# Down product of a gated MLP: seven operand slots, chunks of 3 to 4 pairs, another product order, three homes for h

## The chip, the cores and the metric

The kernel runs on one core of a Trainium2 chip. The metric is the device time of one execution in microseconds (us). Times of the whole program are medians of three runs; everything that is said about single instructions comes from one profiled execution.

Engine names are those of the profile: PE is TensorE (matrix products), DVE is VectorE, ACT is ScalarE, POOL is GpSimd, SP is SyncE, which here only issues DMA transfers. Each engine works through its own instruction list in order. A DMA transfer is issued by one of SP, ACT and POOL and then runs on the core's 16 DMA engines. In the profile, transfers issued by SP are on the queue "hardware_dynamic", those issued by POOL on "software_dynamic".

## What is computed

One decoder layer for 512 prompt positions and 64 sampled positions (576 columns in all). The change concerns the last part only, the gated MLP:

```
def conv_ffn(hn, prev_g, w_gate, w_up, conv_w, conv_b, w_down):
    g = hn @ w_gate                      # 2048 -> 5504
    u = hn @ w_up                        # 2048 -> 5504
    gp = concatenate([prev_g, g], axis=1)
    gc = conv_b + sum(conv_w[j] * gp[:, j:j + T] for j in range(3))
    return (silu(gc) * u) @ w_down       # 5504 -> 2048
...
y = h + conv_ffn(rms_norm(h, g_ffn), ...)
```

All tensors are float32. `h` is the residual stream after attention; it is added to the result.

## The kernel before

**Products in two parts.** A float32 operand is split into a high and a low float32r part (weights `wu`, `wl`; activations `xh`, `xl` or `hi`, `lo`). `multiply` forms wu·xh + wu·xl (lines L1638, L1639), then wl·xh (L1641), so three matmuls of 128x128 by 128x288 per block of 128 rows.

**Seven products for eight.** Gate, up and down use Strassen's scheme in Winograd's form on 2x2 blocks: seven products, numbered 1 to 7, in place of eight. Each needs a combination of the four weight blocks `a11, a21, a22, a12` and one of the activation blocks. `Weights.operand(i)` makes the weight combination: for product 5 the sum `s = a21 + a22` (L1918), then in place `a21 = a11 - a21` (L1919) and `a11 = s - a11` (L1920); for product 6 `s = a12 - a11` (L1924). Then ACT copies the result to `wu` (`upper`, L1626) and DVE subtracts for `wl` (`lower`, L1631). There are four buffers each of `wu` and `wl`, used in turn, so a combination can be made at most four products ahead. `ahead()` makes the next one in the list `todo`, once per product.

**Weight loads.** The four raw blocks of an item go through a ring of five buffers `wrs`, loaded by SP (L1621). `behind` says after which operand the next item's blocks are asked for: after product 1 `a11`, after 6 `a21`, after 7 `a22`, after 4 `a12`. A load into a ring buffer has to wait for the last reader of what was in it.

**Stages.** Gate/up: 43 items, one for each 128 columns of the 5504, each seven products (five for eight of them, whose other two were made earlier). After every second item, `pair` forms the seven activation combinations of the down product for that pair, splits each into a buffer `pp` (two buffers; ACT copy L196, DVE subtraction L199) and stores it to DRAM, `opd[i-1, pair]`, 288 KB, by a DMA issued on POOL (L1785). There are 21 pairs; the last item is odd and has no partner (`oddx`).

Down: the 21 pairs are cut into six chunks `CTS = (4, 4, 4, 3, 3, 3)`, numbered q = 0 to 5. For each chunk, four groups g of 256 output rows (128 from each of two subgroups s, in both row halves), so 24 items. Each item does the seven products for s = 0 and 1: a half product is 12 matmuls for four pairs and 9 for three. An activation operand `ops[q, i]` is loaded from `opd` (`fetch`, L1985, on POOL) into one slot, 1152 KB for four pairs or 864 KB for three, and used by all four groups; in group 3 each slot is free after its product, and the next operand in the list `coming` is loaded into it. The slots are the ten buffers of the gate/up activations that the last gate item frees first (`release(*xops[i])` for products 1, 5, 6, 3, 7).

After each half product, DVE adds the accumulator in PSUM to the rows of `ht` (L2111), which holds h and ends as the output. The PSUM banks are `a` for products 1, 6, 7 and 4 (`pgemm`), `b` for 5 and 3, `c` for 2 (`pone`).

**The hand-over.** Two ring and sum buffers, `room` and `sums`, lie in `x12`, and the scratch of the convolution in `x21`; both are freed together when gate/up ends. `ht` (36 KB in each partition) takes their place, so the last gate item and the first down item have special rules in `behind`, `ahead` stops at the end of the gate list, and a new sum buffer and a fifth ring buffer (`wr4`) are made. `ht` is loaded by eight DMAs on SP (L2060).

The order of instructions on each engine is set by a scheduler that simulates the program; the code gives data, buffers and the order of calls, and the scheduler may run a later instruction earlier.

Of the kernel before, what the change touches and what calls it, by code (L numbers as in the profile page):

```python
# [17 lines left out]
P = 128  # L18
# [29 lines left out]
CQA, CKA, CVA, CFA, CQB, CKB, CVB, CQI, CKI, CWI = (  # L48
    0, 1024, 2048, 3072, 3080, 4104, 4360, 4616, 5640, 5704)
NLATE = 5  # L50
CTS = (4, 4, 4, 3, 3, 3)
PRE = tuple(range(0, 24, 3))


# [1 line left out]
def tile_hymba_step(  # L56
# [1505 lines left out]
    wq_ctx, wq = opened("wq")  # L1562
    fn_ctx, fn = opened("fn")
    wb_ctx, wb = opened("wb")
    ha_ctx, hap = opened("ha", RIGHT)
    hb_ctx, hbp = opened("hb", RIGHT)


    x12, x21 = [hap.tile([P, 8, HALF], F32, name=n) for n in ("x12", "x21")]
    x11, x22 = [hbp.tile([P, 8, HALF], F32, name=n) for n in ("x11", "x22")]  # L1570
    xblk = ((x11, x12), (x21, x22))

# [207 lines left out]
    def pair(n, x, y):  # L1780

        def out(i, t):
            s = prp.tile([P, 2, HALF], F32R, name="pp", bufs=2)
            split(s[:, 0, :], s[:, 1, :], t)
            G.dma_start(opd[i - 1, n], f(s))  # L1785

        b11, b12, b21, b22 = x[:, HV[0]], x[:, HV[1]], y[:, HV[0]], y[:, HV[1]]
        ta, tb = [prp.tile([P, HALF], F32, name=n) for n in ("ta", "tb")]
        V.tensor_sub(ta, b22, b12)
        V.tensor_sub(tb, b12, b11)  # L1790
        out(1, b11)
# [100 lines left out]

    xops = {1: (hi11, lo11), 5: (hi1, lo1), 6: (hi2, lo2), 3: (hi22, lo22), 7: (hi3, lo3), 2: (hi21, lo21), 4: (hi4, lo4)}
    ORDER = (1, 5, 6, 3, 7, 2, 4)
    LATER = (5, 6, 3, 7, 4)
    BANK = {1: "a", 6: "a", 7: "a", 4: "a", 5: "b", 3: "b", 2: "c"}

    class Weights:


        def __init__(self, n, srcs, order=ORDER, odd=False):
            self.n, self.m, self.srcs, self.order, self.odd = n, n + 256 * odd, srcs, order, odd
            self.b, self.ready, self.at = {}, {}, len(items)

            self.behind = {order[0]: ["a11"], 6: ["a21"], 7: ["a22"], 4: ["a12"]}
            if self.at == NF - 1:
                self.behind = {7: ["a11", "a21"], 4: ["a22", "a12"]}
            elif self.at == NF:
                del self.behind[order[0]]

        def load(self, name):
            self.b[name] = wload(*self.srcs[name])
# [1 line left out]
        def operand(self, i):  # L1914
            x, n, m = self.b, self.n, self.n
            s, = sums
            if i == 5:
                V.tensor_add(s[:, :n], x["a21"][:, :n], x["a22"][:, :n])  # L1918
                V.tensor_sub(x["a21"][:, :n], x["a11"][:, :n], x["a21"][:, :n])  # L1919
                V.tensor_sub(x["a11"][:, :n], s[:, :n], x["a11"][:, :n])  # L1920
                if self.odd:
                    V.tensor_copy(s[:, n:self.m], x["a22"][:, n:self.m])
            elif i == 6:
                V.tensor_sub(s[:, :n], x["a12"][:, :n], x["a11"][:, :n])  # L1924
                if self.odd:
                    V.tensor_sub(s[:, n:self.m], x["a12"][:, n:self.m], x["a22"][:, n:self.m])
            if i in (5, 3, 2, 4):
                m = self.m
            src = {1: x["a11"], 5: s, 6: x["a11"], 3: s, 7: x["a21"], 2: x["a12"], 4: x["a22"]}[i]
            h = upper(src, m)  # L1930
            self.ready[i] = (h, lower(src, h, m))
            if self.at == NF - 1 and i == 7:
                wrs[:] = [t for t in wrs if t is not room]
            if self.at + 1 < len(items):
                for name in self.behind.get(i, ()):
                    items[self.at + 1].load(name)

    items = []
    for j in range(NF):
        items.append(Weights(1024, blocks(j), LATER if j in PRE else ORDER))  # L1940
    i0 = 0
    for q, ct in enumerate(CTS):
        odd = q == len(CTS) - 1
        for g in range(4):
            srcs = {}
            for m in range(2):
                cs = slice(m * 1024 + g * 256, m * 1024 + (g + 1) * 256)
                for k in range(2):
                    rows = w_down[:NP * 2 * P, cs].rearrange("(i k p) c -> k p i c", k=2, p=P)
                    at = [(0, rows[k, :, i0:i0 + ct, :])]  # L1950
                    if odd and k == 1:
                        at.append((ct * 256, w_down[NP * 2 * P:, cs]))
                    srcs[f"a{m + 1}{k + 1}"] = at
            items.append(Weights(ct * 256, srcs, odd=odd))
        i0 += ct
    todo = [(w, i) for w in items for i in w.order]
    gate_todo = sum(len(w.order) for w in items[:NF])
    made = [0]

    def ahead(n=1):  # L1960
# [12 lines left out]
    free, ops, coming = [], {}, []  # L1973
    i0 = 0
    for q, ct in enumerate(CTS):
        coming += [(q, i, i0, ct) for i in ORDER]
        i0 += ct

    def fetch():
# [12 lines left out]
    for j in range(NF):  # L1992
# [10 lines left out]
        for i in w.order:  # L2003
# [24 lines left out]
                V.tensor_add(u[:, :HALF], d, p1)  # L2028
            else:
                A.copy(u[:, :HALF], d)  # L2030
            if made[0] <= gate_todo:
                ahead()
            next(pairs, None)
            if j == NF - 1 and i not in (2, 4):
                release(*xops[i])
                if i == 3:
                    fetch()
        for _ in pairs:
            pass
# [3 lines left out]
            next(pairs)  # L2043


    fetch()
    fetch()
    oh, ol = [t.rearrange("p k t -> p (k t)")[:, :NT] for t in xops[2]]
    split(oh, ol, ua)
    oddx = [(oh[:, h], ol[:, h]) for h in HV]  # L2050


    hc_ctx.close()
    ha_ctx.close()
    yb_ctx, yb = opened("yb", RIGHT)
    ht = yb.tile([P, KD, NT], F32, name="ht")
    for g in range(4):
        for m in range(2):
            o = m * 8 + 2 * g
            S.dma_start(ht[:, o:o + 2, :], hdr[o:o + 2].rearrange("k p t -> p k t"))  # L2060
    pr_ctx.close()
    fn_ctx.close()
    ys_ctx, ys = opened("ys")
    sums = [ys.tile([P, 1024], F32, name="sum")]
    wrs.insert(0, ys.tile([P, 1024], F32, name="wr4"))
    items[NF + 1].load("a11")
    ahead(2)

    def outputs(g):

        for t in range(5):
            n = P if t < 4 else NS
            pp = (psum_o if t % 2 else psum_q)()
            for i in range(4):
                T.transpose(pp[:n, i * P:(i + 1) * P], ht[:, i // 2 * 8 + 2 * g + i % 2, t * P:t * P + n], ident)
            yo = ys.tile([P, 512], F32, name="yo", bufs=2)
            (A.copy if t % 2 else V.tensor_copy)(yo[:n, :], pp[:n, :])
            for m in range(2):
# [9 lines left out]
    for q, ct in enumerate(CTS):  # L2088
        for g in range(4):
            w = items[at]  # L2090
            at += 1
            acc = {}
            for i in ORDER:
                bank = BANK[i]
                h, l = w.ready.pop(i)
                x = ops[q, i]
                for s in range(2):
# [5 lines left out]
                    if w.odd and i in (2, 3, 4, 5):  # L2103
                        rows.append((h[:, cs[ct]], l[:, cs[ct]], *oddx[{2: 0, 4: 0, 3: 1, 5: 1}[i]]))
                    multiply(d, rows, i in (1, 5, 2))
                    o1, o2 = 2 * g + s, 8 + 2 * g + s

                    for o, n in {1: ((o1, 0),), 5: ((o2, 1),), 6: ((o1, 1),), 3: ((o1, 1),), 7: ((o2, 1),),
                                 2: ((o1, 0),), 4: ((o2, 0),)}[i]:
                        y = ht[:, o, HV[n]]  # L2110
                        V.tensor_add(y, d, y)  # L2111
                ahead()
                fetch()
                if g == 3:
# [7 lines left out]
        pass  # L2122

    yb_ctx.close()
    xb_ctx.close()
    ys_ctx.close()
    wq_ctx.close()
# [73 lines left out]
```

## Time and profile before

| | |
|---|---|
| median of 3 runs | 2883.14 us (2882.65 to 2883.85) |
| profiled execution | 2880.53 us |
| its span, first to last instruction | 2878.8 us |
| mean granted TensorE clock | 0.983 |
| stages in the span | gate/up ends and down begins at 2310 us; down's last product ends at 2866 us, then the last outputs |

How to read the rows below. A row of windows gives a stretch, its length, and for each engine the busy time and the number of instructions, then the clock granted to TensorE as a share of full speed, the share of the 16 DMA engines that is busy, and GB/s. A row of the waits gives who waited, for whom, the total, how often and the longest. A row of the timeline gives start, duration, engine, line, operation, and in square brackets the idle time before it and what ended it. A row of the chain gives start, duration and what the end of the program was then waiting for. Line numbers are those of the kernel before.

### The profile page before, as it was taken

How to read it: one execution, taken by the hardware profiler on the slowest of the kernel's cores; microseconds unless marked ns; L12 is line 12 of the kernel's file. 1: busy time of each engine (PE TensorE's matmuls, PEld its weight loads, DVE VectorE, ACT ScalarE, POOL GpSimd, SP SyncE). 2: the span in 40 equal slices, each digit the busy share in tenths (PEclk: the TensorE clock that was granted, in tenths of full speed). 3: DMA queues.
4: the chain of work that ended last, by engine and by line, in shares of the span. 5: the costliest groups of instructions: out<-in, count | busy, mean ns of one | idle time of the engine just before them, and what ended most of it. 6: DMA issues, size and time to landing. Idle time of an engine off the chain costs nothing.

```text
span 2878.8 us, 52919 instructions
## 1 busy us (share of the span) xinstructions
PE 2753.7 (96%) x19863; PEld 2639.0 (92%) x19863; DVE 2131.0 (74%) x3783; ACT 1419.9 (49%) x2532; POOL 642.7 (22%) x790
## 2 busy tenths in 40 slices
PE   8999999999999999989999999999999969999898
PEld 7999999999898887879999999999999969988898
DVE  6669598555547666658988888888888857777786
ACT  6546644655655566655445444554555423332232
POOL 1332234325452233320022212111111200000000
PEclk9999999999999999989999999999999989999999
DMA  7233343436547889887555455544445575445543
GB/s 210 63 80 102 99 121 81 113 101 192 160 145 223 271 275 288 268 234 204 145 166 162 149 163 158 156 146 141 143 128 158 162 272 203 129 151 165 167 134 103
DMA packets 526057, 469.98 MB, mean 163 GB/s; under 512 B 35871, under 2 KB 454305, under 8 KB 525289
## 3 DMA queue, kind: packets, MB, share of 16 engines
q1 hardware_dynamic: 499785, 366.77, 44.1%
q0 software_dynamic: 26016, 99.83, 9.5%
q8 instruction: 156, 2.56, 0.4%
q14 instruction: 100, 0.82, 0.1%
HBM read 385.63 MB, written 80.62 MB: 162 GB/s over the span
## 4 chain that ended last, share of the span: by engine, by line
PE 58%; DMA 6%; DVE 4%; issue 1%; ACT 1%; POOL 0%; SPq 0%; DVEq 0%; ACTq 0%; POOLq 0%
PE pgemm L1638 9%; PE pgemm L1639 9%; PE pgemm L1641 8%; PE pone L1638 7%; PE pone L1639 6%; PE pone L1641 6%; DMA wr<-in_w_down_dram 3%; PE pone L1401 2%; PE pgemm L171 2%; PE pgemm L173 2%; PE pgemm L172 2%; DVE wl L1631 2%; PE pout L1471 1%; PE pout L1472 1%; PE pq L1422 1%
## 5 line engine op out<-in xcount | busy, mean ns | idle before, releaser
L171 PE MATMUL pgemm<-xh,wh 128*128 128x288 f32 (+1 forms) x1824 | 551.1, 304 | 5.9 <-ACT wh L151 2.8
L173 PE MATMUL pgemm<-xh,wl 128*128 128x288 f32 (+1 forms) x1824 | 549.6, 302 | 0.7 <-DVE wl L152 0.7
L1626 ACT CAST wu<-wr 128x1024 fp32r<-128x1024 f32 (+1 forms) x311 | 314.3, 1014 | 450.4 <-PE pgemm L1639 190.1
L172 PE MATMUL pgemm<-xl,wh 128*128 128x288 f32 (+1 forms) x1696 | 511.1, 302 | 3.1 <-DVE xl L300 3.1
L1631 DVE TENSOR_TENSOR wl<-wr,wu 128x1024 fp32r<-128x1024 f32 (+1 forms) x311 | 363.2, 1172 | 34.8 <-ACT wu L1626 30.0
L171 PEld LDWEIGHTS pgemm<-xh,wh 128*128 128x128 f32 (+1 forms) x1824 | 345.4, 190 | 14.7 <-ACT wh L151 3.0
L173 PEld LDWEIGHTS pgemm<-xh,wl 128*128 128x128 f32 (+1 forms) x1824 | 345.8, 190 | 6.5 <-issue 1.0
L172 PEld LDWEIGHTS pgemm<-xl,wh 128*128 128x128 f32 (+1 forms) x1696 | 321.7, 190 | 9.7 <-DVE xl L300 4.1
L1638 PE MATMUL pgemm<-xh,wu 128*128 128x288 f32 x1032 | 282.6, 299 | 9.1 <-DVE ht L2111 3.7
L1639 PE MATMUL pgemm<-xl,wu 128*128 128x288 f32 x1040 | 285.1, 297 | 0.0
L1638 PE MATMUL pone<-xh,wu 128*128 128x288 f32 x872 | 238.0, 300 | 5.4 <-ACT wu L1626 5.2
L1639 PE MATMUL pone<-xl,wu 128*128 128x288 f32 x856 | 235.2, 298 | 0.0
L1638 PE MATMUL pgemm<-hi,wu 128*128 128x288 f32 x832 | 227.5, 299 | 3.3 <-DVE ht L2111 2.0
L1639 PE MATMUL pgemm<-lo,wu 128*128 128x288 f32 x792 | 216.9, 297 | 0.0
L1638 PEld LDWEIGHTS pgemm<-xh,wu 128*128 128x128 f32 x1032 | 194.9, 189 | 12.8 <-ACT wu L1626 6.4
L1626 ACT CAST wu<-x 128x1024 fp32r<-128x1024 f32 x126 | 132.2, 1050 | 146.5 <-PE pgemm L1639 83.0
L1785 POOL DMA_DIRECT2D opd<-pp x147 | 79.3, 541 | 558.5 <-DVE pp L199 527.7
L1639 PEld LDWEIGHTS pgemm<-xl,wu 128*128 128x128 f32 x1040 | 197.2, 190 | 0.0
L152 POOL TENSOR_TENSOR wl<-wraw,wh 128x1024 fp32r<-128x1024 f32 (+1 forms) x51 | 122.2, 2395 | 273.9 <-ACT wh L151 266.7
L151 ACT CAST wh<-wraw 128x1024 fp32r<-128x1024 f32 (+1 forms) x122 | 127.2, 1044 | 96.8 <-PE pgemm L172 85.4
L1638 PEld LDWEIGHTS pone<-xh,wu 128*128 128x128 f32 x872 | 165.1, 190 | 6.6 <-ACT wu L1626 6.3
L1641 PE MATMUL pgemm<-xh,wl 128*128 128x288 f32 x1032 | 164.2, 296 | 0.0
(565 smaller groups left out, 7073.9 us busy)
## 6 DMA issues: line engine op xcount, KB each, us to landing
wraw<-in_w_in_dram SPq DMA_DIRECT2D x88, 512.0 KB
wr<-in_w_gate_dram SPq DMA_DIRECT2D x85, 512.0 KB
opd<-pp POOLq DMA_DIRECT2D x147, 288.0 KB, 4.2
wr<-in_w_up_dram SPq DMA_DIRECT2D x69, 512.0 KB
kraw<-in_cache_fox_k_dram SPq DMA_DIRECT2D x128, 256.0 KB
vraw<-in_cache_fox_v_dram SPq DMA_DIRECT2D x128, 256.0 KB
wr<-in_w_down_dram SPq DMA_DIRECT2D x48, 512.0 KB
wr<-in_w_down_dram SPq DMA_DIRECT2D x48, 384.0 KB
```

Source lines behind the costliest of these rows:

```text
L151: A.copy(h[:, :k, :m], raw[:, :k, :m])
L152: (G if share[0] and not u else V).tensor_sub(l[:, :k, :m], raw[:, :k, :m], f(h)[:, :k, :m])
L171: T.matmul(acc[:m, :], h[:, j, :m], xh[:, c], start=kt == 0, stop=False)
L172: T.matmul(acc[:m, :], h[:, j, :m], xl[:, c], start=False, stop=False)
L173: T.matmul(acc[:m, :], l[:, j, :m], xh[:, c], start=False, stop=kt == nk - 1)
L1401: T.transpose(pp[:, g * P:(g + 1) * P], raws[h // 4 * 4 + g][:, h % 4 * P:(h % 4 + 1) * P], ident)
L1626: A.copy(h[:, :n], t[:, :n])
L1631: V.tensor_sub(l[:, :n], t[:, :n], f(h)[:, :n])
L1638: T.matmul(acc, wh, xh, start=start and k == 0, stop=False, skip_group_check=not start)
L1639: T.matmul(acc, wh, xl, start=False, stop=False, skip_group_check=not start)
L1641: T.matmul(acc, wl, xh, start=False, stop=k == len(rows) - 1, skip_group_check=not start)
L1785: G.dma_start(opd[i - 1, n], f(s))
```

## The change

1. `CTS` becomes (3, 4, 4, 4, 3, 3): the first chunk has three pairs, the fourth has four.
2. `x12` gets a pool of its own, `hr`, that stays open to the end. `room` stays in the ring and `sums` stays as it is; `wr4`, the second sum buffer and all special rules in `behind`, `operand` and `ahead` go.
3. `ht` becomes four tiles of four rows each, one for each group g. The first two lie where `hi4`/`lo4` were (pool `yb`), the third where `x21` was (`yc`), the fourth with the outputs (`ys`). Groups 0 and 1 are loaded by SP, 2 and 3 by POOL.
4. The last gate item and all down items make their operands in the order `DOWN = 1 5 6 7 4 3 2` in place of 1 5 6 3 7 2 4.
5. Seven slots in place of ten: those of products 1, 5 and 6 and one of product 3. Whatever is free is fetched at once.
6. The seven stores of the last pair are issued by ACT, not POOL.

```
-CTS = (4, 4, 4, 3, 3, 3)
+CTS = (3, 4, 4, 4, 3, 3)
...
+    hr_ctx, hrp = opened("hr", RIGHT)
-    x12, x21 = [hap.tile([P, 8, HALF], F32, name=n) for n in ("x12", "x21")]
+    x12 = hrp.tile([P, 8, HALF], F32, name="x12")
+    x21 = hap.tile([P, 8, HALF], F32, name="x21")
...
-            G.dma_start(opd[i - 1, n], f(s))
+            (A if n == NP - 1 else G).dma_start(opd[i - 1, n], f(s))
...
+    DOWN = (1, 5, 6, 7, 4, 3, 2)
...
-            if self.at == NF - 1:
-                self.behind = {7: ["a11", "a21"], 4: ["a22", "a12"]}
-            elif self.at == NF:
-                del self.behind[order[0]]
...
-            if self.at == NF - 1 and i == 7:
-                wrs[:] = [t for t in wrs if t is not room]
...
-        items.append(Weights(1024, blocks(j), LATER if j in PRE else ORDER))
+        items.append(Weights(1024, blocks(j), LATER if j in PRE else ORDER if j < NF - 1 else DOWN))
...
-            if made[0] <= gate_todo:
-                ahead()
+            ahead()
             next(pairs, None)
-            if j == NF - 1 and i not in (2, 4):
-                release(*xops[i])
-                if i == 3:
+            if j == NF - 1 and i in (1, 5, 6, 3):
+                release(*xops[i][:1 if i == 3 else 2])
+                while free:
                     fetch()
...
-    ht = yb.tile([P, KD, NT], F32, name="ht")
+    hts = [yb.tile([P, 4, NT], F32, name=f"ht{g}") for g in range(2)]
+    hts.append(yc.tile([P, 4, NT], F32, name="ht2"))
...
+    hts.append(ys.tile([P, 4, NT], F32, name="ht3"))
...
-            S.dma_start(ht[:, o:o + 2, :], hdr[o:o + 2].rearrange("k p t -> p k t"))
+            (S if g < 2 else G).dma_start(hts[g][:, m * 2:m * 2 + 2, :], hdr[o:o + 2].rearrange("k p t -> p k t"))
-    sums = [ys.tile([P, 1024], F32, name="sum")]
-    wrs.insert(0, ys.tile([P, 1024], F32, name="wr4"))
-    items[NF + 1].load("a11")
-    ahead(2)
...
-            for i in ORDER:
+            for i in DOWN:
```

What the change moves is seen at three places of the built program. A row is line, operation, output tile <- input tiles and shape. Up to the last gate item, the two programs have the same order on every engine.

First place: ACT during the last gate item. `pp` is the store buffer of the last pair, `x_17456` (afterwards `x_17459`) the convolution's scratch. Before:

```order
L196 CAST pp<-ta 128x288
L196 CAST pp<-tb 128x288
L1751 COPY x_17456<-pq 18x128
L1768 ACTIVATE x_17456<-gx,cw 128x592
L2030 COPY ua<-pgemm 128x288
L1771 ACTIVATE x_17456<-x_17456 128x592
L196 CAST xh<-ua 128x576
L196 CAST pp<-x_17456 128x288 x2
L1626 CAST wu_17469<-sum 128x1024
```

With the change:

```order
L196 CAST pp<-ta 128x288
L1788 DMA opd<-pp 128x576
L1628 CAST wu_17471<-wr_17468 128x768
L196 CAST pp<-tb 128x288
L1788 DMA opd<-pp 128x576
L1628 CAST wu_17470<-wr_17469 128x768
L1628 CAST wu_17473<-wr_17468 128x768
L1770 ACTIVATE x_17459<-gx,cw 128x592
L1628 CAST wu_17472<-x_17458 128x768
L2027 COPY ua<-pgemm 128x288
```

The stores stand between ACT's own copies, and four operands of the first down item (the rows with 768 columns) stand ahead of the last two copies to `pp`; before, the first one that needs a sum stands behind them.

Second place: SP from the last gate item to the first down items. `ht_28117` and `ht_28118` are the tiles of groups 0 and 1. Before:

```order
L1621 DMA wr_17463<-in_w_down_dram 128x4x256
L1753 DMA out_dram<-x_17456 2x128
L1754 DMA out_dram<-x_17456 16x128
L2060 DMA ht<-hdr 128x2x576 x8
L1621 DMA wr_28112<-in_w_down_dram 128x4x256
L1621 DMA wr_17466<-in_w_down_dram 128x4x256
```

With the change:

```order
L1623 DMA wr_17466<-in_w_down_dram 128x3x256
L1623 DMA wr_17467<-in_w_down_dram 128x3x256
L1623 DMA wr_17469<-in_w_down_dram 128x3x256
L2061 DMA ht_28117<-hdr 128x2x576 x2
L2061 DMA ht_28118<-hdr 128x2x576
L1755 DMA out_dram<-x_17459 2x128
L1756 DMA out_dram<-x_17459 16x128
L1623 DMA wr_17468<-in_w_down_dram 128x3x256
L2061 DMA ht_28118<-hdr 128x2x576
```

Two loads of the second down item (`wr_17467`, `wr_17469`) now stand ahead of h, and three h transfers stand ahead of the next weight load where eight did.

Third place: DVE at the end of the second chunk, from the subtraction that frees the ring buffer for the next item's `a22` (first row) to the sum that reads the loaded block (L1918). The rows with `ht` are the additions after half products. Before:

```order
L1631 TENSOR_TENSOR wl2_17461<-wr4_28112,wu2_17469 128x1024
L2111 TENSOR_TENSOR ht_28097<-pgemm_29607,ht_28097 128x288
L2111 TENSOR_TENSOR ht_28097<-pgemm_29621,ht_28097 128x288
L2111 TENSOR_TENSOR ht_28097<-pone_29637,ht_28097 128x288
L1631 TENSOR_TENSOR wl0_17459<-wr2_17465,wu0_17467 128x1024
L2111 TENSOR_TENSOR ht_28097<-pone_29651,ht_28097 128x288
L1631 TENSOR_TENSOR wl1_17460<-wr0_17463,wu1_17468 128x1024
L1918 TENSOR_TENSOR sum_28111<-wr1_17464,wr4_28112 128x1024
L2111 TENSOR_TENSOR ht_28097<-pgemm_29607,ht_28097 128x288
```

With the change:

```order
L1633 TENSOR_TENSOR wl1_17463<-wr1_17467,wu1_17471 128x1024
L1924 TENSOR_TENSOR x12_17458<-wr3_17469,wr0_17466 128x1024
L2103 TENSOR_TENSOR ht3_28125<-pgemm_29443,ht3_28125 128x288
L2103 TENSOR_TENSOR ht3_28125<-pgemm_29457,ht3_28125 128x288
L1633 TENSOR_TENSOR wl2_17464<-wr2_17468,wu2_17472 128x1024
L2103 TENSOR_TENSOR ht3_28125<-pone_29474,ht3_28125 128x288
L2103 TENSOR_TENSOR ht3_28125<-pone_29488,ht3_28125 128x288
L1633 TENSOR_TENSOR wl3_17465<-x12_17458,wu3_17473 128x1024
L2103 TENSOR_TENSOR ht3_28125<-pgemm_29443,ht3_28125 128x288
L1918 TENSOR_TENSOR x12_17458<-wr0_17466,wr1_17467 128x1024
```

The buffer is freed before the item's first addition (product 1) and the sum stands five additions later, in the middle of product 6; before, it was freed after the additions of product 6 and the sum stood four additions later. On PE the new order is not followed: the scheduler still puts product 3 beside 7, right behind 6, and product 4 with 2 at the end of an item, as before.

More of the change, by code (lines that the diff above doesn't have):

```diff
@@ L1953, in tile_hymba_step @@
                     srcs[f"a{m + 1}{k + 1}"] = at
-            items.append(Weights(ct * 256, srcs, odd=odd))
+            items.append(Weights(ct * 256, srcs, DOWN, odd))
         i0 += ct
     todo = [(w, i) for w in items for i in w.order]
-    gate_todo = sum(len(w.order) for w in items[:NF])
     made = [0]
@@ L1975, in tile_hymba_step @@
     for q, ct in enumerate(CTS):
-        coming += [(q, i, i0, ct) for i in ORDER]
+        coming += [(q, i, i0, ct) for i in DOWN]
         i0 += ct
@@ L2043, in tile_hymba_step @@
             next(pairs)
-    fetch()
-    fetch()
     oh, ol = [t.rearrange("p k t -> p (k t)")[:, :NT] for t in xops[2]]
@@ L2054, in tile_hymba_step @@
     ha_ctx.close()
+    yc_ctx, yc = opened("yc", RIGHT)
     yb_ctx, yb = opened("yb", RIGHT)
-    ht = yb.tile([P, KD, NT], F32, name="ht")
+    hts = [yb.tile([P, 4, NT], F32, name=f"ht{g}") for g in range(2)]
+    hts.append(yc.tile([P, 4, NT], F32, name="ht2"))
+    pr_ctx.close()
+    fn_ctx.close()
+    ys_ctx, ys = opened("ys")
+    hts.append(ys.tile([P, 4, NT], F32, name="ht3"))
     for g in range(4):
@@ L2059, in tile_hymba_step @@
             o = m * 8 + 2 * g
-            S.dma_start(ht[:, o:o + 2, :], hdr[o:o + 2].rearrange("k p t -> p k t"))
-    pr_ctx.close()
-    fn_ctx.close()
-    ys_ctx, ys = opened("ys")
-    sums = [ys.tile([P, 1024], F32, name="sum")]
-    wrs.insert(0, ys.tile([P, 1024], F32, name="wr4"))
-    items[NF + 1].load("a11")
-    ahead(2)
+            (S if g < 2 else G).dma_start(hts[g][:, m * 2:m * 2 + 2, :], hdr[o:o + 2].rearrange("k p t -> p k t"))
     def outputs(g):
@@ L2074, in outputs @@
             for i in range(4):
-                T.transpose(pp[:n, i * P:(i + 1) * P], ht[:, i // 2 * 8 + 2 * g + i % 2, t * P:t * P + n], ident)
+                T.transpose(pp[:n, i * P:(i + 1) * P], hts[g][:, i, t * P:t * P + n], ident)
             yo = ys.tile([P, 512], F32, name="yo", bufs=2)
@@ L2105, in tile_hymba_step @@
                     multiply(d, rows, i in (1, 5, 2))
[L2106 to L2111, printed above, removed]
+                    m, n = {1: (0, 0), 5: (1, 1), 6: (0, 1), 3: (0, 1), 7: (1, 1), 2: (0, 0), 4: (1, 0)}[i]
+                    y = hts[g][:, m * 2 + s, HV[n]]
+                    V.tensor_add(y, d, y)
                 ahead()
@@ L2124, in tile_hymba_step @@
     yb_ctx.close()
+    yc_ctx.close()
+    hr_ctx.close()
     xb_ctx.close()
```

## The prediction

> **What bounds the kernel now.** I read the page first, for the share of PE in the 40 slices:
>
> ```profile
> PE 2753.7 (96%) x19863; PEld 2639.0 (92%) x19863; DVE 2131.0 (74%) x3783; ACT 1419.9 (49%) x2532; POOL 642.7 (22%) x790
> ...
> PE   8999999999999999989999999999999969999898
> ```
>
> PE is the bound in every slice; what can be gained lies where it waits. The digit 6 is the change from gate/up to down. Next the windows, for what gate/up and down cost per matmul (after the stretch and its length: PE busy and its matmuls):
>
> ```profile
> 1423.00:2296.00 873.00, 868.79 (x6501) 867.40 (x6500) 747.85 (x1079) 440.90 (x640) 153.01 (x238) 1.00 0.49 150
> 2310.36:2866.10 555.74, 499.21 (x3687) 493.01 (x3686) 411.78 (x621) 164.96 (x178) 25.61 (x35) 0.96 0.50 164
> ```
>
> Gate/up takes 873.00 / 6501 = 0.1343 us for a matmul at full clock, almost without waits. Down has 3687, which at that pace are 495.1 us; it takes 555.7. So 60.6 us are lost in down, the most that the change can bring. DVE is busy 412 of 556 us and ACT 165, so neither is the bound on the average. The waits of this part (2296 to the end) say who loses it:
>
> ```profile
> DVE sum L1918 <- DMA wr<-in_w_down_dram: 44.2, 19, 7.6
> PE pone L1638 <- ACT wu L1626: 32.3, 8, 25.4
> PE pgemm L1638 <- DVE ht L2111: 23.5, 14, 7.4
> ```
>
> PE waits 55.8 us: one hole of 25.4 and 30.4 in small pieces. The largest of these, by the timeline of PE:
>
> ```profile
> 2526.39 0.58 PE L1638 MATMUL pgemm<-lo,wu 128*128 128x288 f32 x1 [6.44 <-DVE ht L2111]
> 2627.59 0.40 PE L1638 MATMUL pone<-xh,wu 128*128 128x288 f32 x1 [3.15 <-ACT wu L1626]
> 2704.36 0.61 PE L1638 MATMUL pgemm<-xl,wu 128*128 128x288 f32 x1 [7.39 <-DVE ht L2111]
> ```
>
> These three, 17.0 us, stand at the ends of chunks 1, 2 and 3. After such a pause the granted clock (third number from the end) stays low:
>
> ```profile
> 2339.00:2343.00 4.00, 3.91 (x18) 3.91 (x19) 4.00 (x5) 2.14 (x3) 0.00 (x0) 0.57 1.06 394
> ...
> 2526.00:2528.00 2.00, 1.60 (x7) 1.64 (x8) 2.00 (x4) 1.04 (x1) 0.00 (x0) 0.50 1.03 383
> 2528.00:2530.00 2.00, 2.00 (x10) 2.00 (x10) 2.00 (x4) 0.00 (x0) 0.00 (x0) 0.50 0.76 286
> ...
> 2629.00:2631.00 2.00, 2.00 (x11) 2.00 (x10) 2.00 (x5) 0.01 (x1) 0.00 (x0) 0.53 0.29 89
> 2631.00:2633.00 2.00, 2.00 (x12) 2.00 (x11) 1.47 (x4) 0.51 (x1) 0.00 (x0) 0.61 0.50 168
> 2704.00:2706.00 2.00, 1.64 (x7) 1.65 (x8) 2.00 (x4) 0.83 (x1) 0.00 (x0) 0.50 0.77 289
> 2706.00:2708.00 2.00, 2.00 (x11) 2.00 (x11) 1.63 (x3) 0.70 (x1) 0.74 (x1) 0.59 0.14 51
> ```
>
> PE's busy time times the missing clock is 3.91 x 0.43 = 1.7 us after the hole and 0.8 + 1.0 + 0.9 + 0.8 + 0.8 + 0.8 = 5.1 us after the three. With them the waits make 62.6, within 2 us of the 60.6.
>
> **The hand-over.** The chain through the hole, after the last gate product:
>
> ```profile
> 2310.44 20.21 DMA opd<-pp
> 2330.67 0.44 ACT pp L196
> 2331.14 0.47 DVE pp L199
> 2331.66 4.17 DMA ht<-hdr
> ...
> 2336.38 0.45 DVE ht L2111
> 2336.83 1.15 DVE sum L1918
> 2337.99 1.05 ACT wu L1626
> 2339.09 0.61 PE pone L1638
> ```
>
> A store of the last pair takes 20 us. ACT cannot refill `pp` until it has landed, and holds every later copy; the eight h transfers wait for the buffers, the additions for h, and the first down sum stands on DVE behind the additions. The store is slow because it queues on POOL behind operand loads; by queue, from 2290 to 2314 us and for the six stores:
>
> ```profile
> q0 software_dynamic: 1679, 7.22, 81.5%
> q1 hardware_dynamic: 1101, 1.10, 13.6%
> ...
> DMA to landing us min/median/max: 3.1/11.2/21.6
> ```
>
> With the change the seven stores are issued by ACT, out of that queue. SP's loads, on another queue, still moved 1.10 MB beside the 7.22 MB (46 GB/s), so 288 KB need at worst about 6.4 us at that rate and 3.1 at best. A `pp` buffer is reused two stores later, one or two products of 3.2 us (24 matmuls) apart: covered. Seven issues on ACT are not in the trace; POOL's take 0.56 us, so 0 to 3.9 us, on an engine that is 70% idle: taken as 0.
>
> h of group 0 then waits only for product 4 of the last gate item, which ends at 2310.4, and lands 4.2 us later, 2314.6; the addition takes 0.45. Until then PE has products 1 and 5 of the first item (36 matmuls of three pairs, 4.8 us, to 2315.2). So PE waits 0 to 1 us there. Behind the h transfers on SP stands the second item's `a22`, some 3 us later than without them, and DVE's sum waits for it with additions behind: 0 to 6 us. I take 3 in all (range 0 to 10): the first weights, four blocks of the first item and two of the second, stand ahead of h. Of 25.4 + 1.7, **24 us** go.
>
> **The chunk ends.** DVE at the end of chunk 1, and the chain there:
>
> ```profile
> 2509.18 1.23 DVE L1631 TENSOR_TENSOR wl<-wr,wu 128x1024 fp32r<-128x1024 f32 x1
> ...
> 2516.03 1.21 DVE L1631 TENSOR_TENSOR wl<-wr,wu 128x1024 fp32r<-128x1024 f32 x1
> 2524.66 1.22 DVE L1918 TENSOR_TENSOR sum<-wr,wr 128x1024 f32<-128x1024 f32 x1 [7.42 <-DMA wr<-in_w_down_dram]
> ...
> 2510.43 14.13 DMA wr<-in_w_down_dram
> ```
>
> The buffer is free at 2510.4, DVE is at the sum at 2517.2, the load lands at 2524.6, and the additions that would free PSUM stand behind: PE stops. The load is slow because group 3 frees slot after slot for POOL; by queue, from 2514 to 2526 us, against 2495 to 2498 us without operand loads:
>
> ```profile
> q0 software_dynamic: 828, 3.59, 79.5%
> q1 hardware_dynamic: 969, 0.97, 24.3%
> ...
> DMA packets 528, 0.52 MB, mean 175 GB/s; under 512 B 16, under 2 KB 528, under 8 KB 528
> ```
>
> Weights get 0.97 MB in 12 us, 81 GB/s, in place of 175. With `DOWN`, product 7 is fourth and 4 fifth, so `a22` is asked for one operand and `a12` two operands earlier. In the order shown, the buffer for `a22` is free before the first addition of group 3, so before the first slot is free; the load runs alone, 0.52 MB in 3 us. The sum comes five additions later, two and a half products or 8.1 us: no wait. `a12` has twelve additions (19 us; 14.5 with three pairs), the next item's `a22` nine (14.5): all over the 14.1 us of the slowest load. Of 17.0 + 5.1 I leave 3 (range 0 to 22): **19 us** go. The other 13.4 us of small waits come from the same ring (DVE's 19 waits for loads); half may be DVE's order alone, so **6.7 us** go (range 0 to 13.4).
>
> **What is added.** Seven slots: each load has six products until it is needed, 19.3 us with four pairs and 14.5 after the three-pair chunk 0. The landing of all operand loads from 2400 on:
>
> ```profile
> DMA to landing us min/median/max: 5.0/9.3/14.0
> ```
>
> All 29 would be in time; cost 0 (up to 2 us for each of five chunk ends). The first seven, 6.2 MB of three pairs at the 300 GB/s above, take 21 us from about 2292; the last is needed after 2324. The two h tiles on POOL stand ahead of chunk 1's fetches, which start with group 3, some 50 us later: nothing. Chunk sizes are only reordered: same matmuls, same DVE columns.
>
> `wu` and `wl` are used in turn by `DOWN`, but PE does product 4 at the end, so operand 5 of the next item now gets its buffer only when 4 is done. Its copy takes 1.05 us and PE's half product 1 in front of it 1.6, so it just fits. If it never did, 23 item changes at 1.0 us ((32.3 - 25.4) / 7, the mean of the other `wu` waits) cost 23 us; a gain is excluded. ACT is idle enough that I take 3.
>
> Sum: -24 - 19 - 6.7 + 3 = -47 us. From the profiled 2880.5 that is 2833.5; the median of runs stands 2.6 higher, so **2836 us**.
>
> **Rivals.**
> - Weights still late at chunk ends: an item needs 2.1 MB in 22.5 us, 93 GB/s, and gets 81 while operands load; a deficit may only move to a later item. For it: DVE's sums stand early in the list, with additions behind. Against: the three loads' delays are below the new covers. Time: 2836 + 19 + 3 = 2858.
> - The stores gain nothing on ACT, since the same 16 engines are full (81.5 + 13.6%); ACT then waits as before. Against: SP's 46 GB/s in the same stretch. Time: 2836 + 22 = 2858. Here the Trainium skill speaks on both sides. "DMA: Bandwidth & Descriptors", section "Queues, rings and completion order", says that each DMA engine takes turns between queue rows with work and that SP and ACT own a row each; the SP row above agrees, and by it this rival falls. Its section "Issuing engines are not separate DMA queues" says that issuing from several engines saves only the issuer's time; by it the rival's 2858 holds. No run here shows a store from ACT yet.
> - Slower than before: activation operands late for want of slots. In group 3 they land about every 3.9 us (1.18 MB at 299 GB/s); the seventh, 3.2 + 2.5 + 7 x 3.9 = 33 us after the group's start, is needed at 41.7. It decides from 5.1 us each on; at 6.6 (179 GB/s) each of five chunk ends loses 10 us, which eats the 47: 2886. Against: no landing above 14.0, and PE never waited for an operand.
> - The change doesn't do what it says: PE keeps its product order, as the order shows. That removes a feared PSUM wait (6, 7 and 4 share bank `a`) and costs nothing by itself; through the weights it is the first rival.
>
> **How the numbers follow.** Main case 0.70, with 2818 to 2850 as its own range: below is the full 60.6 us, above are half the takings. Weights late 0.13, stores no better 0.07, both 0.04 (2880), operands late 0.06. The range 2818 to 2862 holds the main case and both single rivals. 0.2% (6 us) is about what can be told from no change: faster 0.70 + 0.13 + 0.07 + 0.01 = 0.91, same 0.03, slower 0.06.
>
> **What would show it.** Right: PE's hole after the last gate item under 10 us; stores landing in under 7; no wait of over 3 us by PE at chunk ends, and DVE's waits for weight loads well under 44 us; no granted clock of 0.5 in down. Wrong: PE waiting for a DMA of `opd`; many `wu` waits of about 1 us in front of product 5; sums still waiting 5 us or more.

## The result, and the profile after

The changed kernel takes 2831.33 us (median of four runs, 2829.11 to 2834.27), the kernel before 2882.89 (2880.69 to 2883.85): ratio 0.9823, 95% interval 0.9806 to 0.9840, 51.6 us less. The forecast was 2836, with a range of 2818 to 2862. The profiled execution takes 2832.15 us, its span is 2830.4. The lines of the changed kernel differ a little: matmuls L1640, L1641 and L1643, `wu` L1628, `wl` L1633, additions to h L2103, h loads L2061, operand loads L1982; the new stores stand in L1788, the sums still in L1918 to L1924.

The page of the changed kernel, busy time and the 40 slices:

```profile
PE 2750.0 (97%) x19863; PEld 2636.1 (93%) x19863; DVE 2132.7 (75%) x3783; ACT 1418.8 (50%) x2532; POOL 640.9 (23%) x787
...
PE   8999999999999999999999999999999999999998
```

The digit 6 is gone, and the busy times are nearly the old ones: what went are waits, not work. The waits from 2296 us to the end:

```profile
DVE x L1918 <- DMA wr<-in_w_down_dram: 19.6, 8, 4.4
PE pgemm L1640 <- DVE ht L2103: 6.2, 5, 3.6
PE pgemm L1640 <- issue: 5.1, 2, 4.1
ACT pp L196 <- DMA opd<-pp: 2.9, 2, 2.7
```

PE waits 11.3 us in place of 55.8, and never for a `wu` copy; DVE waits 19.6 us at the sum for weight loads into `wr`, and 4.0 for those into the ring buffer that now stays in `x12`, in place of 44.2. Two waits of PE are left that cost something, at the hand-over and at the start of the last chunk (PE's timeline):

```profile
2323.07 0.61 PE L1640 MATMUL pgemm<-hi,wu 128*128 128x288 f32 x1 [3.60 <-DVE ht L2103]
...
2729.96 0.58 PE L1640 MATMUL pgemm<-xh,wu 128*128 128x288 f32 x1 [4.07 <-issue]
```

After both, the granted clock is at half (windows of the changed kernel):

```profile
2323.00:2327.00 4.00, 3.93 (x16) 3.93 (x17) 1.67 (x5) 0.00 (x0) 0.02 (x1) 0.50 1.06 386
2730.00:2732.00 2.00, 2.00 (x8) 2.00 (x9) 2.00 (x4) 1.23 (x2) 0.00 (x0) 0.50 1.03 387
```

Executions differ before down begins (in the profiled ones of the table below this mark stands anywhere from 2310.6 to 2325.4 us), so I also compare the down stage alone: from ACT's copy of product 4 of the last gate item to the end of the span. These are the two copies, of the kernel before and of the changed one:

```profile
2310.57 0.40 ACT L2030 COPY ua<-pgemm 128x288 f32<-128x288 f32 x1 [1.96 <-PE pgemm L1641]
```

```profile
2315.56 0.40 ACT L2027 COPY ua<-pgemm 128x288 f32<-128x288 f32 x1 [0.76 <-PE pgemm L1643]
```

2878.8 - 2310.6 = 568.2 us before, 2830.4 - 2315.6 = 514.8 after: 53.4 us less. The same measure for every run (the hole is PE's waiting between the last gate products and the second down item):

| kernel | median us (runs) | ratio to before, 95% interval | down stage us | hole us |
|---|---|---|---|---|
| before | 2882.89 (4) | 1 | 568.2 | 25.4 |
| changed | 2831.33 (4) | 0.9823, 0.9806 to 0.9840 | 514.8 | 3.6 |
| before, stores on ACT | 2862.49 (5) | 0.9925, 0.9895 to 0.9954 | 542.1 | 7.2 + 5.1 |
| before, order `DOWN` | 2850.91 (4) | 0.9883, 0.9850 to 0.9916 | 535.6 | 25.6 |
| before, both of these | 2850.82 (4) | 0.9894, 0.9875 to 0.9912 | 528.1 | 10.9 + 5.3 |
| before, 7 slots, first chunk of 3 | 2867.56 (4) | 0.9952, 0.9933 to 0.9970 | 546.8 | 12.8 |
| changed, stores on POOL | 2833.70 (4) | 0.9827, 0.9795 to 0.9859 | 518.5 | 4.1 |
| changed, old order | 2869.26 (9) | 0.9951, 0.9933 to 0.9969 | 547.9 | 0.8 + 7.6 |
| changed, ten slots | 2842.87 (4) | 0.9856, 0.9829 to 0.9884 | 523.2 | 9.4 + 1.8 |
| changed, stores on POOL, h 0 at `x21` | 2846.91 (4) | 0.9877, 0.9852 to 0.9902 | 526.6 | 16.8 |
| changed, old chunk sizes | 2847.84 (4) | 0.9873, 0.9848 to 0.9898 | 528.2 | 7.0 + 8.4 |
| changed, sizes 3 3 4 4 4 3 | 2828.11 (5) | 0.9808, 0.9787 to 0.9829 | 510.3 | 3.5 |
| the same, odd split on POOL | 2826.64 (5) | 0.9808, 0.9792 to 0.9824 | 508.0 | 3.7 |
| changed, once more | 2836.34 (5) | 0.9843, 0.9827 to 0.9860 | 516.2 | 3.9 |

Each ratio is to runs of the kernel before on the same chip (medians 2880.7 to 2884.1). The two measurements of the changed kernel differ by 5.0 us in the medians and 1.4 in the down stage: smaller differences between two rows show nothing by themselves.

### The profile page after: what moved, and what is told of

Its sections match the earlier page's. It is cut to its first block, busy times and chain, and to the rows that moved or that the text cites. A ratio compares the mean times of both kernels' runs of the same rounds, so it can differ in the third digit from the quotient of the medians.

```text
span 2830.4 us, 52901 instructions
## 1 busy us (share of the span) xinstructions
PE 2750.0 (97%) x19863; PEld 2636.1 (93%) x19863; DVE 2132.7 (75%) x3783; ACT 1418.8 (50%) x2532; POOL 640.9 (23%) x787
## 4 chain that ended last, share of the span: by engine, by line
PE 62%; DMA 3%; DVE 2%; issue 1%; ACT 1%; SPq 0%; POOL 0%; ACTq 0%; DVEq 0%; POOLq 0%
PE pgemm L1640 10%; PE pgemm L1641 10%; PE pgemm L1643 9%; PE pone L1640 7%; PE pone L1641 7%; PE pone L1643 7%; PE pone L1401 2%; PE pgemm L173 2%; PE pgemm L171 2%; PE pgemm L172 2%; PE pout L1471 1%; PE pout L1472 1%; DMA wr<-in_w_down_dram 1%; DMA vraw<-in_cache_fox_v_dram 1%; PE pq L1423 1%
## 5 line engine op out<-in xcount | busy, mean ns | idle before, releaser
L1628 ACT CAST wu<-wr 128x1024 fp32r<-128x1024 f32 (+1 forms) x287 | 291.5, 1019 | 403.1 <-PE pgemm L1641 192.8
L1633 DVE TENSOR_TENSOR wl<-wr,wu 128x1024 fp32r<-128x1024 f32 (+1 forms) x287 | 337.1, 1179 | 33.6 <-ACT wu L1628 30.1
L1628 ACT CAST wu<-x 128x1024 fp32r<-128x1024 f32 (+1 forms) x198 | 201.7, 1022 | 258.3 <-PE pgemm L1641 135.9
L1640 PE MATMUL pgemm<-hi,wu 128*128 128x288 f32 x1024 | 280.4, 298 | 5.0 <-DVE ht L2103 3.6
L1640 PE MATMUL pgemm<-xh,wu 128*128 128x288 f32 x992 | 271.6, 299 | 11.7 <-issue 5.1
L1633 DVE TENSOR_TENSOR wl<-x,wu 128x1024 fp32r<-128x1024 f32 (+1 forms) x198 | 233.4, 1182 | 14.9 <-ACT wu L1628 10.5
L1640 PE MATMUL pone<-xh,wu 128*128 128x288 f32 x880 | 240.6, 299 | 1.3 <-ACT wu L1628 1.3
L1641 PE MATMUL pone<-xl,wu 128*128 128x288 f32 x880 | 241.4, 297 | 0.0
L1641 PE MATMUL pgemm<-lo,wu 128*128 128x288 f32 x856 | 232.8, 296 | 0.0
L1641 PE MATMUL pgemm<-xl,wu 128*128 128x288 f32 x824 | 224.1, 296 | 0.0
L1640 PEld LDWEIGHTS pgemm<-xh,wu 128*128 128x128 f32 x992 | 187.2, 189 | 14.9 <-issue 5.5
L1640 PEld LDWEIGHTS pgemm<-hi,wu 128*128 128x128 f32 x1024 | 193.8, 189 | 5.5 <-DVE ht L2103 3.8
L1788 POOL DMA_DIRECT2D opd<-pp x140 | 75.5, 541 | 524.3 <-DVE pp L199 495.5
L1640 PEld LDWEIGHTS pone<-xh,wu 128*128 128x128 f32 x880 | 166.6, 190 | 1.5 <-ACT wu L1628 1.5
```

The source lines that it names most:

```text
L1628: A.copy(h[:, :n], t[:, :n])
L1633: V.tensor_sub(l[:, :n], t[:, :n], f(h)[:, :n])
L1640: T.matmul(acc, wh, xh, start=start and k == 0, stop=False, skip_group_check=not start)
L1641: T.matmul(acc, wh, xl, start=False, stop=False, skip_group_check=not start)
L1788: (A if n == NP - 1 else G).dma_start(opd[i - 1, n], f(s))
```

## The experiments

**One edit alone, or one taken back: stores and order.** My theory was that the stores on ACT close the hole and the order closes the chunk ends. The kernel before with only the stores moved:

```
-            G.dma_start(opd[i - 1, n], f(s))
+            (A if n == NP - 1 else G).dma_start(opd[i - 1, n], f(s))
```

> The kernel before (2882.9 us) with the seven stores of the last pair issued by ACT, and nothing else changed. Theory A (the hand-over hole comes from stores queued behind POOL's operand loads): the stores land in under 7 us in place of 20, the hole of 25.4 us after the last gate item shrinks to under 10, and the time is 2859 us (2853 to 2868). Theory B (the hole comes from something else, h or the first sums, or all transfers share the same full engines): stores land as late as before, the hole stays above 18 us, the time is 2883 (2877 to 2886).

Its waits for the stores, and PE's timeline:

```profile
ACT pp L196 <- DMA opd<-pp: 1.8, 1, 1.8
```

```profile
2328.24 0.61 PE L1638 MATMUL pone<-xl,wu 128*128 128x288 f32 x1 [7.19 <-ACT wu L1626]
2337.22 2.29 PE L1641 MATMUL pone<-xl,wl 128*128 128x288 f32 x8 [5.09 <-DVE wl L1631]
```

ACT waits 1.8 us for the stores in place of 21.6, but a hole of 12.3 us stays. Theory A holds for the time, not for the hole, which it had under 10, and not for the stores, which it had landing in under 7 us: by the semaphore updates in the traces six of them land 6.6 to 10.3 us after their issue, against 3.1 to 21.6 in the kernel before. The reverse, the changed kernel with `G.dma_start` for all stores:

> The changed kernel (2831.3 us) with the stores of the last pair back on POOL. Theory A: stores land in about 20 us again, ACT stands at the copies into pp with the weight copies of the first down item behind, the hole returns to 15 to 25 us, and the time is 2853 us (2845 to 2858). Theory B (in the changed kernel h in three places and the early weight loads carry the hand-over): hole stays under 8 us, the time is 2832 (2827 to 2837).

Theory B: 2833.7 us. The stores are on POOL's queue again (issue, number, KB, median us to landing; 2292 to 2320 us), and PE hardly notices:

```profile
opd<-pp POOLq DMA_DIRECT2D x4, 288.0 KB, 11.4
```

```profile
2324.07 0.61 PE L1640 MATMUL pgemm<-hi,wu 128*128 128x288 f32 x1 [4.07 <-DVE ht L2103]
```

They do not land in 20 us again, as theory A had it: six of them land in 5.7 to 11.4 us from POOL, and in 5.7 to 10.0 from ACT in the changed kernel. So in the changed kernel something else has already taken the queue in front of the stores away. DVE's first addition to h now waits for h itself, as the part on a better version shows further:

```profile
2323.55 0.82 DVE L2103 TENSOR_TENSOR ht<-pgemm,ht 128x288 f32<-128x288 f32 x2 [0.32 <-DMA ht<-hdr]
```

The order, alone in the kernel before:

```
+    DOWN = (1, 5, 6, 7, 4, 3, 2)
...
-            items.append(Weights(ct * 256, srcs, odd=odd))
+            items.append(Weights(ct * 256, srcs, DOWN, odd))
...
-        coming += [(q, i, i0, ct) for i in ORDER]
+        coming += [(q, i, i0, ct) for i in DOWN]
...
-            for i in ORDER:
+            for i in DOWN:
```

> The kernel before (2882.9 us) with the products of the down items, and the operand loads, in the order 1 5 6 7 4 3 2; ten slots, chunk sizes and the hand-over as before. Theory A (the order alone takes away the chunk-end waits and half of the small ones): DVE's waits for weight loads at the sums go from 44 us to under 20, no PE wait above 3 us at chunk ends, the time is 2860 us (2855 to 2866). Theory B (the order only moves the deficit, or the seven slots and the chunk sizes do it): chunk-end waits stay at 10 to 17 us in all, the time is 2880 (2874 to 2885).

Theory A, and more than it said: 30 us in the medians (same chip), 32.6 in the down stage. The hole is untouched at 25.56; PE's other waits fall from 30.4 us to 8.0, and DVE's waits at the sum (L1919 here) are

```profile
DVE sum L1919 <- DMA wr<-in_w_down_dram: 15.6, 9, 3.4
```

against 44.2. The reverse, the changed kernel with `DOWN = ORDER`:

> The changed kernel (2831.3 us) with the old order 1 5 6 3 7 2 4 in the down product (and in the last gate item); slots, chunk sizes and hand-over stay. On DVE's list the sums then have 1 to 11 additions between the freeing of their buffer and themselves, in place of 5 to 9. Theory A: chunk-end waits of PE come back to 10 to 20 us with the slow clock behind them, DVE's waits for weight loads above 35 us, the time is 2853 us (2845 to 2860). Theory B (the order gave nothing, slots and placement did): PE's waits at chunk ends stay under 3 us each, the time is 2832 (2827 to 2838).

Theory A, and again larger: 38 us. At the end of chunk 0 its SP, DVE and PE read

```profile
2402.05 0.37 SPq L1623 DMA_DIRECT2D wr<-in_w_down_dram  x1
```

```profile
2402.31 0.81 DVE L2103 TENSOR_TENSOR ht<-pgemm,ht 128x288 f32<-128x288 f32 x2
2414.83 1.23 DVE L1918 TENSOR_TENSOR x<-x,wr 128x1024 f32<-128x1024 f32 x1 [11.71 <-DMA wr<-in_w_down_dram]
```

```profile
2416.48 0.61 PE L1640 MATMUL pgemm<-xh,wu 128*128 128x288 f32 x1 [10.96 <-DVE ht L2103]
```

The load for the sum is asked for 1.1 us before DVE comes to it, and DVE stands 11.7 us until it lands beside the operand loads: the mechanism the prediction gave for the chunk ends, shown by putting it back.

**What else closed the hole.** Since the stores were not it, three edits were taken back one at a time. Ten slots:

```
-            if j == NF - 1 and i in (1, 5, 6, 3):
-                release(*xops[i][:1 if i == 3 else 2])
+            if j == NF - 1 and i in (1, 5, 6, 3, 7):
+                release(*xops[i])
```

> The changed kernel (2831.3 us) with ten operand slots in place of seven (products 1, 5, 6, 3 and 7 of the last gate item release both of their places). Theory A (the number of slots gives and costs nothing: operands are in time with seven, and ten load the same bytes): 2832 us (2827 to 2837), PE's waits at the hand-over under 6 us. Theory B (part of the gain at the hand-over comes from three operand loads, 2.6 MB or some 9 us at 300 GB/s, that seven slots keep away from the stores, h and the first weights): the hole at the hand-over grows by 4 to 9 us, the time is 2839 us (2836 to 2846).

Theory B, with 9.36 us of hole. The reason is in the queues, from 2320 to 2328 us (packets, MB, share of the engines; the stores' queue is left out), of the changed kernel and then of the one with ten slots:

```profile
q1 hardware_dynamic: 1660, 2.71, 93.3%
...
q0 software_dynamic: 2, 0.00, 0.2%
```

```profile
q0 software_dynamic: 506, 2.18, 71.9%
q1 hardware_dynamic: 507, 0.94, 32.8%
```

With seven slots POOL's queue is empty at 2320 and SP's h and weights have the engines to themselves; with ten it is still at work and they get three tenths of the bytes. The way from there to PE runs through ACT (its timeline with ten slots):

```profile
2327.19 0.33 ACTq L1788 DMA_DIRECT2D opd<-pp  x1
2327.83 0.43 ACT L196 CAST pp<-x 128x288 fp32r<-128x288 f32 x1 [7.42 <-DMA ht<-hdr]
```

In this program the store that ACT issues at 2327.19 has the same semaphore as an h load of SP's, and its issue waits until that load has landed (2327.1 by the semaphore's updates). ACT's last copy into `pp`, DVE's subtraction and the additions to h stand behind it. Moving the stores to ACT thus tied ACT to SP's loads, which the prediction did not see.

The chunk sizes, `CTS = (4, 4, 4, 3, 3, 3)` in the changed kernel, do the same with 8.3 MB in place of 6.2:

> The changed kernel (2831.3 us) with the chunk sizes 4 4 4 3 3 3 as before the change. Theory A (sizes hardly matter; the first seven operand loads are 8.3 MB in place of 6.2 and land some 7 us later, against first products that are a third longer): 2833 us (2828 to 2840). Theory B (the smaller first chunk is needed for the first operands to be in time): PE waits for an operand load (opd) within the first item, 5 to 10 us, 2840 us (2837 to 2846).

The time is theory B's, and slower still; its reason is not: PE waited for no operand load. The first hole, 7.0 us, ends with an addition that waits 1.0 us for h, and the next additions wait 3.7 more for it; the second, 8.4 us, stands behind a sum that waits for the second item's weights. Both loads are on SP's queue:

```profile
2333.60 0.82 DVE L2103 TENSOR_TENSOR ht<-pone,ht 128x288 f32<-128x288 f32 x2 [3.67 <-DMA ht<-hdr]
...
2347.66 1.23 DVE L1918 TENSOR_TENSOR x<-wr,wr 128x1024 f32<-128x1024 f32 x1 [10.85 <-DMA wr<-in_w_down_dram]
```

Then h's place, with the stores on POOL:

```
-    hts = [yb.tile([P, 4, NT], F32, name=f"ht{g}") for g in range(2)]
-    hts.append(yc.tile([P, 4, NT], F32, name="ht2"))
+    hts = [yc.tile([P, 4, NT], F32, name="ht0")]
+    hts += [yb.tile([P, 4, NT], F32, name=f"ht{g}") for g in (1, 2)]
```

> The changed kernel with the stores of the last pair back on POOL, which alone gave 2833.7 us, and with the first tile of h put where x21 stood (the second and third where hi4 and lo4 stood), so that h of group 0 waits again for the last pair's copies. Theory A (it is h's place that cut the hand-over loose from the stores: either of the two edits is enough to take most of the hole away): the first h load is issued at least 6 us later, after the last copy into pp, the hole grows from 4 to 10 to 18 us, and the time is 2844 us (2839 to 2851). Theory B (the hole went with the first weights asked for earlier and with fewer operand loads; the place of h does not matter): hole under 6 us, 2834 us (2829 to 2838).

Theory A's time (2846.91) and hole, against 2833.7 and 4.07 with h where the change puts it. Its chain through the hole names the last reader of `x21`:

```profile
2318.47 11.86 DMA out_dram<-x
...
2330.48 6.55 DMA ht<-hdr
...
2337.15 0.47 DVE ht L2103
...
2337.66 0.61 PE pgemm L1640
```

Not the last pair's copies, as I wrote, but the store of the convolution's last rows, which lie in `x21` too: it takes 11.9 us. h's place is a cause, by another reader than I named.

**Backlog alone, and two edits together.** If what is queued on POOL sets the hole, cutting the bytes in the kernel before must shorten it, with stores and h as they were. `CTS` and `release` of the changed kernel in the kernel before:

> The kernel before (2883 us) with seven slots in place of ten and with the chunk sizes 3 4 4 4 3 3; order of products, stores on POOL, h's place and the weights as before. At the hand-over POOL's queue then holds 7 loads of 0.88 MB, 6.2 MB, in place of 10 of 1.18 MB, 11.8 MB. Theory A (the hole of 25.4 us is the time that this backlog takes: 5.6 MB less at the 390 GB/s of that queue are 14 us): hole 11 us (6 to 16), the other waits as before or somewhat more, time 2870 us (2864 to 2878). Theory B (any loads ahead of the stores, and h's place behind the last copies, make the hole): hole 20 us or more, time 2881 us (2877 to 2887).

Theory A: hole 12.81 us, 14.0 us faster. Slots and sizes are changed together here; the two runs above separate them. Its chain has the same links as before; the store takes 12.2 us in place of 20.2:

```profile
2310.28 12.20 DMA opd<-pp
...
2323.48 4.71 DMA ht<-hdr
```

Stores on ACT and the order together, in the kernel before:

> The kernel before (2883 us) with two edits together: the last pair's stores on ACT, and the down items in the order 1 5 6 7 4 3 2; ten slots, four-pair first chunk, h in one tile as before. Alone they gave 18 and 30 us. Theory A (the two stand for the whole change, their gains add up): 2834 us (2829 to 2838). Theory B (the backlog of ten operand loads still holds h and the first weights back as in the run with the stores alone, holes of 7.2 and 5.1 us in place of 3.6): 2843 us (2838 to 2850).

Not theory A: 2850.8 us, as much as the order alone in the medians (7.5 us less in the down stage), where the two gains added would be 2834. It is theory B's cause, at more than its price. The hole is 10.9 + 5.3 us, and its chain shows SP's transfers slow behind ten operand loads of 1152 KB:

```profile
2306.27 19.29 DMA wr<-in_w_down_dram
...
2329.71 9.61 DMA ht<-hdr
```

**A better version.** What is left at the last chunk's start is DVE standing at a sum again, with few additions between (DVE's timeline of the changed kernel):

```profile
2721.18 0.46 DVE L2103 TENSOR_TENSOR ht<-pgemm,ht 128x288 f32<-128x288 f32 x1 [0.73 <-PE pgemm L1643]
2726.07 0.96 DVE L1918 TENSOR_TENSOR x<-wr,x 128x768 f32<-128x768 f32 x1 [4.43 <-DMA wr<-in_w_down_dram]
```

The chunk before it has three pairs. With `CTS = (3, 3, 4, 4, 4, 3)` it has four:

> The changed kernel (2831.3 us) with chunk sizes 3 3 4 4 4 3, so that the end of the fifth chunk, where PE still waits 4.07 us and then runs 2 us at a lower clock, has four pairs: its four additions between the freed weight buffer and the sum then last a third longer. Theory A (the remaining wait is the sum's load not covered in a three-pair chunk): that wait goes under 2 us, no new one above 2 us, 2827 us (2823 to 2831). Theory B (three-pair chunk ends lose it wherever they stand, now after the second chunk): a wait of 3 to 6 us at the second chunk's end, 2831 us (2828 to 2835).

2828.11 us, and no wait of PE at that place: theory A for the wait, though another end now has 2.87 us, more than the 2 it allowed; the time lies in both theories' ranges. The rest of the hole I put down to DVE's own list (the chain of the changed kernel):

```profile
2320.06 0.95 DVE wl L1633
2321.01 0.68 DVE xl L199
...
2321.73 0.44 ACT pp L196
...
2322.19 0.46 DVE pp L199
2322.65 0.38 DVE ht L2103
```

so `xl` of the odd tile went to POOL, on top of the new sizes: `split(oh, ol, ua, lo=G)`.

> The changed kernel with chunk sizes 3 3 4 4 4 3 (2828.1 us alone) and the lower part of the odd tile's split (0.75 us on DVE, ahead of the first h additions) made by POOL. Theory A (DVE's own queue is what is left of the hand-over hole): hole 2.7 us in place of 3.5, time 2827 us (2822 to 2830). Theory B (something else is late there by as much, or POOL's slower subtraction delays its h loads): hole 3.4 us or more, 2829 us (2826 to 2835).

Theory B for the hole: 3.70 us. POOL takes 1.59 us for `xl`, and DVE's two `wl` subtractions beside it take 3.03 in place of 1.83 (POOL and DVE of this kernel, then DVE of the changed one):

```profile
2316.91 1.59 POOL L199 TENSOR_TENSOR xl<-ua,xh 128x576 fp32r<-128x576 f32 x1 [8.73 <-ACT xh L196]
```

```profile
2316.29 3.03 DVE L1633 TENSOR_TENSOR wl<-x,wu 128x768 fp32r<-128x768 f32 x2 [0.70 <-ACT wu L1628]
```

```profile
2319.18 1.83 DVE L1633 TENSOR_TENSOR wl<-x,wu 128x768 fp32r<-128x768 f32 x2 [0.70 <-ACT wu L1628]
```

But DVE's list is not what its chain names. It runs from a weight load to ACT's issue of a store, as with ten slots, and to the copy behind that issue:

```profile
2309.36 8.84 DMA wr<-in_w_down_dram
2318.28 0.33 ACTq L1788
...
2318.92 0.44 ACT pp L196
2319.39 0.46 DVE pp L199
2319.84 0.38 DVE ht L2103
```

And a third limit stands beside these two: h itself. In the changed kernel SP asks for the first h load at 2315.55, and its next weight load waits for that one to land (SP's waits from 2316 to 2324 us, then its timeline):

```profile
SPq L1623 <- DMA ht<-hdr: 3.7, 1, 3.7
```

```profile
2315.55 1.39 SPq L2061 DMA_DIRECT2D ht<-hdr  x3
...
2322.57 0.37 SPq L1623 DMA_DIRECT2D x<-in_w_down_dram  x1
```

So the load takes 7.0 us, and DVE's first addition also starts at 2322.57. With the split on POOL the same two stand together at 2319.76, and with the stores on POOL the addition waits for h, as shown above. What is left of the hole is set by SP's loads at least as much as by DVE's list, and shortening that list alone could not close it.

> The changed kernel as it is, on the same chip as the version with the sizes 3 3 4 4 4 3: 2831 us (2828 to 2835), PE's wait at the end of the fifth chunk 3 to 6 us again if that wait belongs to the kernel and not to one execution.

2836.34 us (2835.30 to 2839.26), slower than the range I gave, with 4.62 us at the last chunk's start again: that wait belongs to the kernel. Against it on the same chip the version with the sizes 3 3 4 4 4 3 and the odd split on POOL takes 2826.64 (2822.40 to 2826.95): 9.7 us or 0.3% faster. With the sizes the wait at the last chunk's start is gone, and with it the slow clock there; that the split adds anything is not shown.

## Why the prediction was right, and where its reasons were not

- **The floor and the bound.** Right: of PE's 55.8 us of waits, 44.5 went.
- **The hand-over, 24 us.** The size nearly holds: 25.4 to 3.6, with 2.7 us lost to the clock (windows of 2 us, by the prediction's rule) in place of 1.7, 20.8 net. The reason was a half. "Out of that queue" was taken for the cure, and it is not: with it alone 12 us of hole stay, and without it the changed kernel is 2.4 us slower in the medians, less than two measurements of one kernel differ, and 3.7 in the down stage, of which 0.5 us is the hole. The step that failed is the one that carried the 46 GB/s of SP's loads to the stores only: from ACT they land in 5.7 to 10.0 us, not in 3.1 to 6.4, and the same backlog holds back h and the first weights. The change shortens the backlog twice, by three slots fewer and by a first chunk of three pairs.
- **The issues on ACT, taken as 0.** Each takes 0.33 us, but an issue can stand until a load of SP's has landed: 7.4 us of ACT's time with ten slots.
- **"Seven slots: cost 0", "chunk sizes are only reordered".** Wrong: each is worth more than the stores. Taken back, they cost 11.5 and 16.5 us in medians (of which up to 5 can be the difference between measurements), 8.4 and 13.4 in the down stage. The prediction worked out that 6.2 MB take 21 us from 2292, asked whether the operands are in time, and did not ask who stands beside them. (Its row of landings holds 32 loads, not 29; nothing hangs on it.)
- **h of group 0.** That it waits for product 4 only is right, and is worth 8.1 us of the down stage with the stores on POOL. Its landing was mis-sized: 4.2 us were taken from the kernel before, and the first load takes 7.0. PE's products last until 2319.5 and h lands at 2322.5, so PE waits 3.6 us in place of 0 to 1. The chain names DVE's and ACT's last splits, which end at the same moment.
- **Chunk ends, 19 us.** The mechanism is shown twice. At the ends of chunks 1, 2 and 3 PE waits under 1 us each, with no slow clock. The first rival, weights still late, survives at the end of chunk 4 only: 4.07 us and 2.4 of slow clock. With 1.6 us left at the three ends, 14.0 net against 19.
- **Small waits, 6.7 us.** Mis-sized: 13.4 fell to 2.0, 11.4 us. That half of them were DVE's order alone was a guess; the order alone took all of PE's waits but the hole from 30.4 us to 8.0. With the chunk ends this makes 25 us for the order's part, where the order alone gave 30.
- **Operand 5's buffer, 3 us.** Nothing: no wait of PE for a `wu` copy in the rows.
- **The sum.** -20.8 - 14.0 - 11.4 is -46.2 against -47, and the down stage lost 53.4. The total came so near because the misses have both signs (the hand-over and the chunk ends gave 8.2 us less than forecast, the small waits and operand 5's buffer 7.7 more), which is luck. Most of the other 7.2 us are in PE's busy time: from the mark to the last product it fell from 499.2 us (3687 matmuls) to 491.5 (3680). The 7 matmuls, which stand ahead of the mark in the changed kernel, are 1 us of this and the clock, counted above, nearly 2. The remaining 5 us are matmuls that take less time at full clock, and I did not trace why.
- **The rivals.** "The stores gain nothing on ACT" was priced at 2858; with the stores on POOL the kernel takes 2833.7, so that price was wrong whichever rule holds. Operands late for want of slots: no row shows PE waiting for one, and more slots made it slower.
- **The signs.** Hole under 10, and DVE's waits for weight loads well under 44: yes. Stores landing in under 7: no, four of the six took longer. No wait over 3 us at chunk ends and no clock of 0.5: each fails at the last chunk, the second at the hand-over too. Of the signs of being wrong none came: PE waited for no load from `opd` and no `wu` copy, and DVE's longest wait at a sum was 4.4 us.

## What to carry to other kernels

Count the bytes that are queued ahead of a stage's first needs, for every queue and not only for the transfer that ends the chain: a prefetch that is early enough for itself can be what makes the next stage late, and fewer buffers can be faster. When one engine waits in order, ask how many instructions stand between freeing a buffer and needing its next content, and reorder the work to raise that number. Edits that relieve the same wait do not add up, so take each out alone before giving it the credit.

## What the runs showed of the hardware

- Two busy DMA queues are served packet for packet: 506 and 507 packets in the 8 us above, and 488 and 486 in the same stretch with the old chunk sizes, so they share by packet size. With ten slots the operands' packets carry 4.3 KB (2.18 MB / 506) and leave h and weights, at 1.9 KB, 0.94 MB of 3.12. In the Trainium skill, "DMA: Bandwidth & Descriptors", section "Queues, rings and completion order", each DMA engine takes turns between rows packet by packet; these rows agree. Its section "Issuing engines are not separate DMA queues" would have moving the stores save only issue time; ACT's wait for them fell from 21.6 to 1.8 us in the kernel before, so the measurement decides against it there; in the changed kernel, whose backlog is short, the hole is 4.1 us with the stores on POOL and 3.6 with them on ACT.
- The clock fell to half after each pause of PE of 3.15 us or more in down that was looked at. After shorter ones it depends: after 2.55 (seven slots in the kernel before) and 2.82 us (old order, as after 2.65 in its last gate item) it did, after 2.83 (the order alone), 2.87 (sizes 3 3 4 4 4 3) and 3.00 us (old order) it did not, nor after 2.22 (before).
- Beside a subtraction of 1.59 us on POOL, DVE's two took 3.0 us in place of 1.8, once. In the Trainium skill, "GPSIMD Engine Reference", section "Specifications", lists POOL's SBUF interfaces as shared with VectorE, contended by DVE instructions with two SBUF inputs; these are such.
